# Value products of single units flushed one at a time, and indexer scores rectified in place in PSUM

## The chip, the cores and the metric

The kernel runs on one core of a Trainium2 chip. The metric is the device time of one execution, in microseconds. The time of before is the median of three runs; the profile is of a separate execution. Engines are named as in the profile: PE (TensorE) with its weight loads PEld, DVE (VectorE), ACT (ScalarE), POOL (GpSimd) and SP, which issues transfers.

## What is computed

One layer of a decoder trunk on x of 512 tokens by 1024 channels, in float32. One input projection feeds three causal token mixers. The parts that matter here, cut from the reference:

```python
u = einsum('bsd,de->bse', x, w_in) + b_in          # all projections
# B) sparse attention: an indexer picks 128 keys per query
rel   = relu(einsum('bthd,bsd->bths', iqb, ik))    # 8 index heads of 32
score = einsum('bths,bth->bts', rel, iwb)          # weighted sum over heads
_, idx = top_k(where(causal, score, NEG), topk)
o_b = softmax(q k[idx] / 8) v[idx]                 # 8 heads of 64, one key head
# C) compressed-block, selected-block and window branches, gated and summed
o_c = gb[..., 0:1] * o_cmp + gb[..., 1:2] * o_s + gb[..., 2:3] * o_w
# merge, output projection, LayerNorm
m = g[:, :, 0] * (y_a @ w_pa) + g[:, :, 1] * (y_b @ w_pb) + g[:, :, 2] * (y_c @ w_pc)
out = layernorm(ALPHA * x + m @ w_o)
```

A) is a pooling mixer with windows of 2 to 16. With 512 tokens the selected-block branch takes all blocks, so only the indexer's top-k changes which keys are attended.

## The kernel before

Every f32 product is made of three products of a high and a low part (`mm3`, L67 to L70; groups `d`, `pp` and `wo` in the profile). A projection of 128 channels (`dense`) has 8 steps of three matmuls of 128x512. Weights come through `load_w`: a DMA into a staging tile, a copy of the high part on ACT (L93), a subtraction for the low part (L95), on POOL while the attention runs.

PE's instructions stand in the order in which the program issues them (`manual_schedule` for PE). The instructions of the other engines and of the DMA queues are placed by the compiler's own schedule. The program writes PE's order by weaving two things: the attention, and a stream `F` of projections, compressions and merges, of which `F.step(n)` issues the next n steps as filler.

**The indexer.** `index_scores(j)` (L285 to L301) makes the scores of query block j = 1, 2, 3: for each of 8 heads a matmul into a PSUM tile `is` of the pool `pq` (4 buffers of one bank), a rectification on ACT into an SBUF tile `rel` (L292, from the tag `b` with 6 buffers), and a multiply-add on DVE into the sums `acc` (L294 for the first head, L296 for the others). Two filler steps stand after each head. Beside it run the compressions of keys and values (`compress_in`, `bk`, `bkl`; `compress_mid`, `cpk`) and the scale of the values (`vscales`). The top-k on the sums is 16 rounds of `MAX8` and `MATCH_REPLACE8` on DVE for each block (L305, L306), spread over the attention that follows.

**The attention.** Work is cut into units. A "c" unit (group g, query block j, branch br) is a selected-block or window attention; the two branches of one (g, j) add into the same accumulator. A "b" unit (g, j) is the sparse attention of four heads, with an accumulator of its own. There are 16 "c" units, then 8 "b" units in the order b00, b01, b02, b03, b10 to b13 (g, then j). A unit consists of one or two sub-units. `front` (L422) makes the scores `qk` (L442), softmax and the probabilities `p` (L461, L463), and a transposing DMA on SP into `pt` (L470; tag `pt`, 2 buffers). `back` (L472) makes the value products on PE (L480): for each of j + 1 blocks of keys three times two matmuls in f16. `finish` (L533) is one DVE instruction that reads the accumulator and writes `yc` or `yb`.

The two accumulators that take turns (`psum_acc`) are halves of one tile, `ACC`, of 2 KB per partition:

```python
ACC = pv.tile([128, 2, 2, 128], F32, name="acc2")
```

Units whose `front` is issued wait in the list `backs` with the count of sub-units at that time. `flush(limit)` (L781) takes two units at a time, when the second one lies at least LAG = 2 sub-units back, issues both units' `back` and `finish`, then filler steps. At the end `flush(1000)` takes the rest and puts 12 filler steps before each pair.

Of the kernel before, what the change touches and what calls it, by code (L numbers as in the profile page):

```python
# [7 lines left out]
F32 = mybir.dt.float32  # L8
# [26 lines left out]
def trunk(ctx, tc, a, out, dbg=None):  # L35
# [12 lines left out]
    def big(tag, name, dt=F32, shape=(128, 2, 512)):  # L48
        return bp.tile(list(shape), dt, tag=tag, name=name, bufs=BUFS[tag])
# [4 lines left out]
    def dps(name):  # L54
        return pd.tile([128, 512], F32, tag="pd", name=name)

    def qps(name):
        return pq.tile([128, 512], F32, tag="pq", name=name)
# [42 lines left out]
    ps = qps("idle")  # L101
# [183 lines left out]
    def index_scores(j):  # L285
        n = (j + 1) * 128
        acc = cp.tile([128, n], F32, name=f"acc{j}")
        for h in range(8):
            ps = qps(f"is{j}{h}")[:, :n]
            nc.tensor.matmul(ps, QI[h][:, (j - 1) * 128:j * 128], KI[:, :n], start=True, stop=True)  # L290
            rel = big("b", "rel", F32, (128, 512))[:, :n]
            nc.scalar.activation(rel, ps, AF.Relu)  # L292
            if h == 0:
                nc.vector.tensor_scalar(acc, rel, IW[:, j, 0:1], None, op0=OP.mult)  # L294
            else:
                nc.vector.scalar_tensor_tensor(acc, rel, IW[:, j, h:h + 1], acc, op0=OP.mult, op1=OP.add)  # L296
            yield
        dg = acc[:, j * 128:n]
        nc.vector.tensor_add(dg, dg, cmask[:, 384:512])
        dbg(f"score{j}", acc)  # L300
        negm[j] = acc  # L301
# [231 lines left out]
    def finish(acc, j, Z, y):  # L533
        c = slice(j * 128, j * 128 + 128)
        nc.vector.scalar_tensor_tensor(y[:, :, c], acc, yscale, Z[:, :, c], op0=OP.mult, op1=OP.mult)
# [4 lines left out]
    def psum_acc():  # L540

        turn[0] ^= 1
        return ACC[:, turn[0]]
# [105 lines left out]
    def split_y(br, src):  # L649
        YS[br] = []  # L650
        for g in range(2):
            h, l = big("t", f"yh{br}{g}", F32R), big("t", f"yl{br}{g}", F32R)
            split(h, l, src[g])
            YS[br].append((h, l))
# [77 lines left out]
    for n in (2, 1, 1, 1, 1, 1, 2):  # L732
        for _ in range(n):
            st.step()
        for _ in range(n):
# [11 lines left out]
               [(early_g, 2, d) for d in range(1, 4)] +  # L747
               ["c1", (f_qb, 1, 0), (f_qb, 1, 1), (f_zb, 1, 0), (f_zb, 1, 1)] + [(merge, 2, d) for d in range(KT)])
    ix = Stream([(index_scores, j) for j in (1, 2, 3)])
    while ix.step():  # L750
        F.step(2)
# [4 lines left out]
    def tk(n):  # L756
        tkn[0] += n
        while rounds and tkn[0] >= 1:
            tkn[0] -= 1
            fn, j = rounds.pop(0)  # L760
            fn(j)

    def tk_until(j):
        while (topk_end, j) in rounds:
            fn, i = rounds.pop(0)
            fn(i)
# [10 lines left out]
    backs = []  # L777
    accs, cmps = {}, {}
    nsub = 0

    def flush(limit):  # L781

        while backs and (limit == 1000 or len(backs) > 1 and backs[1][0] <= limit):
            pair, n = backs[:2], 0
            del backs[:2]
            if limit == 1000:
                F.step(12)
            for _, un, (kind, g, j, br) in pair:
                if kind == "c":
                    F.until(("vscales",), ("compress_v",), ("f_zc", g, 0), ("f_zc", g, 1))  # L790
                else:
                    F.until(("f_zb", g, 0), ("f_zb", g, 1))
            for _, un, (kind, g, j, br) in pair:
                for _ in un.back(br == 0):
                    n += 1
                if kind == "b":
                    finish(un.acc, j, zb[g], YB[g])
                elif br == 1:
                    cmps[g, j].back(un.acc)
                    finish(un.acc, j, zc[g], YC[g])  # L800
                    if j == 0:
                        flags.add(f"c{g}")
                        if g == 1:
                            split_y(2, YC)
            F.step(0.3 * n)

    for w in work:
        kind, g, j, br = w
        if kind == "c":
            if br == 0:  # L810
                accs[w[:3]] = psum_acc()
            F.until(("compress_k",), *([("f_kk", g)] if g else []), *([("f_qc", g, e) for e in range(2)] if g else []))
            if j == 3 and br == 0:
                YC.append(big("t", f"yc{g}"))
            gv = GS[:, j, :].rearrange("p (h b) -> p h b", b=3)
            if br == 0:
                cmps[g, j] = Compressed(g)
            un = Unit(f"c{g}{j}{br}", accs[w[:3]], j, qc[g], kk[g][br], cmask[:, (3 - j) * 128:],
                      1 + 2 * br + g, gv[:, 4 * g:4 * g + 4, 1 + br], None if br else cmps[g, j])
        else:  # L820
            F.until(("f_qb", g, 0), ("f_qb", g, 1))
            if j == 0:
                YB.append(big("t", f"yb{g}"))
            if j:
                tk_until(j)
            un = Unit(f"b{g}{j}", psum_acc(), j, qb[g], KB[0], cmask[:, 384:] if j == 0 else negm[j],
                      0, None)
        for u in range(un.nsub):
            for _ in un.front(u):
                F.step(3.25)  # L830
            with tc.issue_after(un.last.ins):
                tk(1.7)
            nsub += 1
            F.step(2)
            flush(nsub - LAG)
        backs.append((nsub, un, w))
    flush(1000)
    F.rest()
    POOL[0] = False
# [60 lines left out]
    for t in range(NT):  # L900
        last = t == NT - 1
        for c0, c1 in ((512, 768), (768, 1024)) if last else ((512, 1024),):
            ps = dps("wo")
# [14 lines left out]
        if not last:  # L918
            c = cs.pop()
# [82 lines left out]
```

## Time and profile before

| | |
|---|---|
| median of 3 runs | 537.79 us (534.98 to 538.72) |
| the profiled execution | 536.65 us |
| its span, first to last instruction | 534.9 us |
| PE busy | 510.4 us |
| DVE / ACT / POOL busy | 380.2 / 278.4 / 218.5 us |
| mean granted TensorE clock | 0.982 of 2.4 GHz |

Busy time of PE counts modelled ends of pipelined matmuls; the start times of successive matmuls are the better measure inside a stretch. Idle time of an engine is put down to the instruction that released it.

### The profile page before, as it was taken

The page shows a single profiled execution, that of the slowest core. Times are in us where ns is not written, and L with a number is a line of the kernel's source. Part 1 is how long each engine was busy: PE and PEld are TensorE (multiplying, and loading weights), DVE is VectorE, ACT ScalarE, POOL GpSimd, SP SyncE. Part 2 cuts the span into 40 slices and gives each one's busy share as a digit, 9 for nine tenths or more (in the row PEclk, how much of TensorE's full clock was granted, in tenths as well). Part 3 has the DMA queues.
Part 4 walks back from the last instruction along what each step waited for, and adds up shares of the span by engine and source line. Part 5 has one row for each costly group of instructions (what it writes and reads, how often), then busy time and mean ns, then how long its engine had stood idle before and what let it go on. Part 6 is the DMA issues. An engine that isn't in the chain of part 4 may idle for free. (4 is left out here: it accounts for less than half of the span.)

```text
span 534.9 us, 7764 instructions
## 1 busy us (share of the span) xinstructions
PE 510.4 (95%) x2718; PEld 423.7 (79%) x2718; DVE 380.2 (71%) x928; ACT 278.4 (52%) x561; POOL 218.5 (41%) x190
## 2 busy tenths in 40 slices
PE   8999999999999998999998995999899999999993
PEld 5899878888888886788887884887787888887883
DVE  5774798898769898997898879565653345554276
ACT  6783465667655666565546564575553245342000
POOL 0425433436553756153534534227651212116043
PEclk9999989999999999999999998899999999999997
DMA  8622331363854434364545636256444435463012
GB/s 286 256 79 80 112 126 60 87 148 86 183 139 123 119 85 117 63 181 124 140 121 104 132 110 145 49 138 138 119 119 134 141 137 187 148 205 110 1 69 89
DMA packets 82135, 66.72 MB, mean 125 GB/s; under 512 B 67184, under 2 KB 68656, under 8 KB 82096
## 3 DMA queue, kind: packets, MB, share of 16 engines
q1 hardware_dynamic: 74912, 40.54, 28.5%
q0 software_dynamic: 7184, 25.69, 16.1%
q8 instruction: 21, 0.34, 0.3%
q14 instruction: 18, 0.15, 0.1%
HBM read 47.87 MB, written 2.10 MB: 93 GB/s over the span
## 5 line engine op out<-in xcount | busy, mean ns | idle before, releaser
L68 PE MATMUL d<-xh,w_h 128*128 128x512 f32 (+1 forms) x424 | 167.5, 395 | 2.6 <-ACT z L153 2.2
L69 PE MATMUL d<-xl,w_h 128*128 128x512 f32 (+1 forms) x424 | 165.8, 391 | 0.0
L70 PE MATMUL d<-xh,w_l 128*128 128x512 f32 (+1 forms) x424 | 165.5, 390 | 0.0
L95 POOL TENSOR_TENSOR w_l<-w_st,w_h 128x1024 fp32r<-128x1024 f32 x41 | 99.5, 2428 | 127.1 <-ACT w_h L93 120.4
L68 PEld LDWEIGHTS d<-xh,w_h 128*128 128x128 f32 x424 | 80.5, 190 | 18.3 <-ACT z L153 2.6
L70 PEld LDWEIGHTS d<-xh,w_l 128*128 128x128 f32 x424 | 80.3, 189 | 16.9
L69 PEld LDWEIGHTS d<-xl,w_h 128*128 128x128 f32 x424 | 80.4, 190 | 14.1
L93 ACT ACTIVATE w_h<-w_st 128x1024 fp32r<-128x1024 f32 x53 | 56.2, 1060 | 36.9 <-DMA w_st<-in_wt_dram 20.5
L449 ACT ACTIVATE qkc<-qkc,nb 128x512 f32<-128x512 f32 (+3 forms) x64 | 32.0, 501 | 49.8 <-DVE nb L444 32.0
L95 POOL TENSOR_TENSOR wp_l<-wp_st,wp_h 128x512 fp32r<-128x512 f32 x16 | 20.8, 1297 | 48.3 <-ACT wp_h L93 48.3
L641 POOL TENSOR_TENSOR m<-m,tg 128x512 f32<-128x512 f32 x12 | 17.5, 1457 | 54.2 <-DVE tg L615 54.0
L463 DVE SCALAR_TENSOR_TENSOR pc<-qkc,r,pc 128x512 f16<-128x512 f32 (+3 forms) x64 | 32.4, 544 | 8.2 <-ACT pc L461 7.9
L461 ACT ACTIVATE pc<-qkc,r 128x512 f16<-128x512 f32 (+3 forms) x64 | 29.5, 525 | 15.1 <-DVE r L457 7.2
L444 DVE CUSTOM_DVE_ANT_0 qkc<-qkc,cmask 128x512 f32<-128x512 f32 (+3 forms) x64 | 31.2, 493 | 2.9 <-PE qkc L442 2.5
L449 ACT ACTIVATE qkb<-qkb,nb 128x128 f32<-128x128 f32 (+3 forms) x32 | 16.0, 499 | 23.1 <-DVE nb L444 22.8
L92 POOL DMA_DIRECT2D w_st<-in_wt_dram x41 | 23.3, 569 | 9.9 <-POOL w_l L95 5.9
L70 PE MATMUL wo<-woh,ml 128*128 128x512 f32 (+1 forms) x72 | 26.4, 367 | 0.6 <-DVE ml L65 0.6
L69 PE MATMUL wo<-wol,mh 128*128 128x512 f32 (+1 forms) x72 | 26.3, 366 | 0.0
L68 PE MATMUL wo<-woh,mh 128*128 128x512 f32 (+1 forms) x72 | 26.3, 365 | 0.0
L306 DVE MATCH_REPLACE8 acc<-m,acc 128x256 f32<-128x256 f32 (+2 forms) x48 | 25.9, 541 | 0.0
L305 DVE MAX8 m<-acc 128x8 f32<-128x256 f32 (+2 forms) x48 | 25.2, 548 | 0.1
L68 PE MATMUL pp<-yh,wp_h 128*128 128x512 f32 x64 | 25.1, 392 | 0.0
(249 smaller groups left out, 1015.3 us busy)
## 6 DMA issues: line engine op xcount, KB each, us to landing
w_st<-in_wt_dram POOLq DMA_DIRECT2D x41, 512.0 KB, 3.7
w_st<-in_wt_dram SPq DMA_DIRECT2D x12, 512.0 KB, 4.4
wp_st<-in_wp_dram POOLq DMA_DIRECT2D x16, 256.0 KB, 3.0
wo_st<-in_wo_dram SPq DMA_DIRECT2D x8, 512.0 KB, 3.5
xst<-in_xT_dram SPq DMA_DIRECT2D x8, 256.0 KB, 4.8
wp_st<-in_wp_dram SPq DMA_DIRECT2D x8, 256.0 KB, 2.6
z<-in_x_dram SPq DMA_DIRECT2D x4, 512.0 KB, 5.1
wvst<-in_wve_dram SPq DMA_DIRECT2D x4, 320.0 KB, 7.1
```

The lines of the kernel that those rows point to most:

```text
L68: nc.tensor.matmul(ps, wh, rh, start=start, stop=False)
L69: nc.tensor.matmul(ps, wh, rl, start=False, stop=False)
L70: nc.tensor.matmul(ps, wl, rh, start=False, stop=stop)
L92: (nc.gpsimd if POOL[0] else nc.sync).dma_start(st, src)
L93: nc.scalar.activation(h[:, :n], st, AF.Copy)
L95: eng.tensor_sub(l[:, :n], st, f(h[:, :n]))
L305: nc.vector.max(m8, negm[j])
L306: nc.vector.match_replace(negm[j], m8, negm[j], MARK)
L444: nc.vector.tensor_tensor_reduce(sc[i], sc[i], self.mask, -0.125, 3e38, OP.add, OP.min, nb[:, i:i + 1])
L449: nc.scalar.activation(sc[i], sc[i], AF.Exp, scale=-1.0, bias=nb[:, i:i + 1], accum_out=den[:, i:i + 1])
L461: nc.scalar.activation(p[:, 0, i], sc[i], AF.Copy, scale=r[:, i:i + 1])
L463: self.last = nc.vector.scalar_tensor_tensor(p[:, 1, i], sc[i], r[:, i:i + 1], p[:, 0, i], op0=OP.mult, op1=OP.subtract)
```

## The change

`flush` takes two units only where the kind is "c", whose two units share an accumulator; a "b" unit is flushed alone, as soon as it lies two sub-units back. The filler steps ahead of a group in the last flush are 8 in place of 12. In `index_scores` the rectified score is written over the score in its PSUM tile instead of into `rel` in SBUF.

```diff
@@ index_scores
             nc.tensor.matmul(ps, QI[h][:, (j - 1) * 128:j * 128], KI[:, :n], start=True, stop=True)
-            rel = big("b", "rel", F32, (128, 512))[:, :n]
+            rel = ps
             nc.scalar.activation(rel, ps, AF.Relu)
@@ flush
-        while backs and (limit == 1000 or len(backs) > 1 and backs[1][0] <= limit):
-            pair, n = backs[:2], 0
-            del backs[:2]
+        while backs and (limit == 1000 or len(backs) >= backs[0][3] and backs[backs[0][3] - 1][0] <= limit):
+            pair, n = backs[:backs[0][3]], 0
+            del backs[:len(pair)]
             if limit == 1000:
-                F.step(12)
-            for _, un, (kind, g, j, br) in pair:
+                F.step(8)
+            for _, un, (kind, g, j, br), _ in pair:
...
-            for _, un, (kind, g, j, br) in pair:
+            for _, un, (kind, g, j, br), _ in pair:
@@ the loop over the units
-        backs.append((nsub, un, w))
+        backs.append((nsub, un, w, 2 if kind == "c" else 1))
```

## Rows read from the trace of the kernel before

**Rows 1.** The page, busy time of each engine and its share of the span.

```profile
PE 510.4 (95%) x2718; PEld 423.7 (79%) x2718; DVE 380.2 (71%) x928; ACT 278.4 (52%) x561; POOL 218.5 (41%) x190
```

**Rows 2.** PE's waits: us in total, times, longest us.

```profile
PE acc L480 <- DVE yb L535: 8.0, 4, 5.5
PE d L68 <- ACT z L153: 2.2, 1, 2.2
...
PE cpk L69 <- DVE bkl L65: 1.2, 1, 1.2
...
PE wo L70 <- DVE ml L65: 0.6, 1, 0.6
```

**Rows 3.** Windows of 20 us: PE, PEld, DVE, ACT, POOL busy, granted clock, DMA.

```profile
60.00:80.00 20.00, 18.84 (x114) 15.96 (x113) 19.23 (x28) 11.97 (x20) 8.22 (x6) 0.91 0.40 132
...
320.00:340.00 20.00, 14.55 (x71) 11.55 (x70) 15.25 (x34) 8.65 (x19) 5.86 (x4) 0.83 0.56 126
```

**Rows 4.** PE's timeline, first pair of "b" units: start, length, line, operands.

```profile
328.22 0.28 PE L480 MATMUL acc<-ptb,vh 128*64 128x256 f16 x2
333.95 0.42 PE L480 MATMUL acc<-ptb,vh 128*64 128x256 f16 x2 [5.45 <-DVE yb L535]
...
337.64 0.39 PE L68 MATMUL d<-xh,w_h 128*128 128x512 f32 x1
```

**Rows 5.** PE's timeline, third pair of "b" units.

```profile
382.21 0.28 PE L480 MATMUL acc<-ptb,vh 128*64 128x256 f16 x2
383.91 0.30 PE L480 MATMUL acc<-ptb,vh 128*64 128x256 f16 x2 [1.42 <-DVE yb L535]
...
385.95 0.39 PE L68 MATMUL d<-xh,w_h 128*128 128x512 f32 x1
```

**Rows 6.** PE's timeline, last pair of "b" units.

```profile
405.44 0.39 PE L70 MATMUL d<-xh,w_l 128*128 128x512 f32 x1
...
406.12 0.39 PE L70 MATMUL d<-xh,w_l 128*128 128x512 f32 x1
406.44 0.30 PE L480 MATMUL acc<-ptb,vh 128*64 128x256 f16 x2
...
408.20 0.30 PE L480 MATMUL acc<-ptb,vh 128*64 128x256 f16 x2 [0.58 <-DVE yb L535]
...
409.39 0.30 PE L480 MATMUL acc<-ptb,vh 128*64 128x256 f16 x2
...
409.96 0.39 PE L69 MATMUL d<-xl,w_h 128*128 128x512 f32 x1
```

**Rows 7.** DVE's timeline, the read of the first "b" unit's sums.

```profile
333.43 0.47 DVE L535 SCALAR_TENSOR_TENSOR yb<-acc,yscale,zb 128x256 f32<-128x256 f32 x1
```

**Rows 8.** PE's second score of b02; the last transpose on SP; its time to landing.

```profile
321.03 0.51 PE L442 MATMUL qkb<-kb,bq 128*128 128x384 f32 x2
...
400.06 1.56 SPq L470 DMA_TRANSPOSE ptb<-pb  x1
...
ptb<-pb SPq DMA_TRANSPOSE x1, 3.6
```

**Rows 9.** DVE's and POOL's timelines in the index stage.

```profile
57.38 0.48 DVE L296 SCALAR_TENSOR_TENSOR acc<-rel,iw,acc 128x256 f32<-128x256 f32 x1 [1.02 <-ACT rel L292]
...
59.54 2.46 DVE L296 SCALAR_TENSOR_TENSOR acc<-rel,iw,acc 128x256 f32<-128x256 f32 x1
...
72.58 2.98 DVE L334 SCALAR_TENSOR_TENSOR bk<-d,bias,small 64x496 f32<-64x496 f32 x4
...
59.33 2.39 POOL L95 TENSOR_TENSOR w_l<-w_st,w_h 128x1024 fp32r<-128x1024 f32 x1 [4.24 <-ACT w_h L93]
...
72.39 2.40 POOL L95 TENSOR_TENSOR w_l<-w_st,w_h 128x1024 fp32r<-128x1024 f32 x1 [3.49 <-ACT w_h L93]
```

**Rows 10.** PE's 12th index score; DVE's step for the 8th.

```profile
68.28 0.34 PE L290 MATMUL is<-ki,qi 128*128 128x384 f32 x1
...
67.97 0.49 DVE L296 SCALAR_TENSOR_TENSOR acc<-rel,iw,acc 128x256 f32<-128x256 f32 x1
```

## The prediction

> **What bounds the kernel now.** I read the page's busy table first: TensorE (PE) is busy for 95% of the span [rows 1], so time can only come out of PE's idle stretches and out of stretches at a low granted clock. PE's program order is fixed by hand, so whatever one of its instructions waits for delays everything behind it. The second view is the list of PE's waits [rows 2]: the largest entry is a value product (`acc`, L480) waiting for a VectorE read of the accumulator (`yb`, L535), 8.0 us in 4 waits, the longest 5.5. The others are single waits of 2.2 and 1.2 us. Third, the windows of 20 us [rows 3]: in 320:340 PE is busy for 14.55 us and its clock averages 0.83; in 60:80 there is a small dip of the same kind (18.84 us, 0.91). Fourth, PE's timeline at the four waits [rows 4 to 6]: each lies between two groups of products of one pair of "b" units. PE issues the first unit's products, then must wait until VectorE (DVE) has read that unit's sums, since the second unit's sums lie in the other half of the same bank-sized tile. All four come before 410 us, and later there is one PE wait of 0.6 us (`wo`, on `ml`) [rows 2], so what is saved should reach the end.
>
> **Edit 1, "b" units flushed singly: what it removes.** Products of one group start 0.054 us apart (24 products from 408.20 to the last pair at 409.39: 1.19/22) [rows 6]. The pair at 328.22 should thus be followed at 328.33, and the next one starts at 333.95: a gap of 5.62, 0.17 more than the 5.45 that the row gives as idle [rows 4]. The pair at 382.21 gives 1.59 against 1.42, again 0.17 [rows 5]. Four gaps are therefore 8.0 + 4 x 0.17 = 8.7 us. The long one also costs clock: after it, PE's 12 products, 2 scores and 3 projection matmuls take from 333.95 to 337.64, 3.69 us [rows 4], while the same seventeen after the short gap take from 383.91 to 385.95, 2.04 us [rows 5]. That is 1.65 us at the lower of the two clock levels. Removed in all: 8.7 + 1.65 = 10.35 us.
>
> **What it adds.** Four pairs become eight stretches, so four more changes between f32 projections and f16 products. Three projection matmuls take 0.68 us (405.44 to 406.12), 0.227 each. Entering a stretch costs 406.44 - 406.12 - 0.227 = 0.09; leaving it, from the last pair at 409.39 to the second f32 matmul at 409.96, costs 0.57 - 0.11 - 0.227 = 0.23 [rows 6]. That is 0.32 each and 1.3 us for four. Bounds: zero, if these pauses exist inside the old gaps too, and twice 0.32 each. I take 1.3.
>
> **What it moves.** The first unit's products of each pair go one sub-unit forward. Unit b00 now has them just before the score matmul of 321.03 [rows 8], and b01 keeps about its old place at 328. So some 7 us of projections lie between them. What decides is when DVE reads b00's sums. In the old order that read ran at 333.43, 5.1 us after the products ended at 328.33, because DVE was behind with top-k and softmax work [rows 4, 7]. With the same lag the read would begin at 321.4 + 5.1 = 326.5 and end before 328: no wait left, with 1 us to spare. The remaining pairs had gaps of 1.59 and 0.75, so DVE was hardly behind there, and their new distance is again a sub-unit of about 6 us. If a read is late, all of PE's stream queues behind that product. The early products issue no transfer, but they free the buffer for the next unit's transposed probabilities sooner; the transposing DMAs on SP can only move forward. Their own inputs are in place: the last unit's transpose is issued at 400.06 and takes 3.6 us, so it lands at 403.7, 2.7 us ahead of its group's start at 406.44 [rows 6, 8]. There the new order has b12's 18 products and 0.9 step in between but 8 steps in place of 12. That is 3.1 steps of 0.68 less and 1.3 us more (18 x 0.054 + 0.32), 0.8 us less cover out of 2.7: still enough. If that cover failed, the price would be the shortfall alone. The number of steps before the end of the filler stream is the same in sum, only spread differently: nothing.
>
> **Edit 2, the rectified scores stay in PSUM.** Nothing is removed from PE. ScalarE writes, and DVE reads, a PSUM tile instead of an SBUF one, 24 times, and each of the four PSUM buffers is held until DVE is done instead of until ScalarE is done. No row shows this very form, so I bound it. DVE's step on 256 columns takes 0.48 us from SBUF [rows 9]. A step with its input in PSUM ran at 2.98/4 = 0.75 us for 496 columns, which is the same rate with a fixed part. So the duration stays. One of the 24, at 59.54, took 2.46 us: it began 0.2 us after a GpSimd subtraction of 2.39 us (59.33 to 61.72) and ended 0.3 after it. Yet the four steps with PSUM input at 72.58 lay beside just such a subtraction (72.39 to 74.79) and were not held up [rows 9].
>
> The Trainium skill, "SBUF — State Buffer", section "Who interferes with whom", says that a VectorE instruction with two SBUF inputs shares a read port with GpSimd while one with a single SBUF input does not; both rows agree. By this rule the held-up step would fall from 2.46 to 0.48 us; without it edit 2 would give nothing.
>
> What hangs on that step is the scale of the values, then the weights of the compression, and then PE's 1.2 us wait for `bkl` [rows 2]. Gain at most: that wait and the clock beside it, 1.2 + 0.09 x 20 = 3.0 us [rows 2, 3]. Against it stands the held buffer: score n+4 must wait for DVE's step n. The closest place in the old trace: the 12th score starts at 68.28, and the 8th score's step begins at 67.97 and lasts 0.49, so it would free the buffer at 68.46, 0.2 us too late [rows 10]. Loss with DVE's order unchanged: 0.2 us, which the wait for `bkl` then absorbs. Since DVE is the late engine there, PE can't run far ahead even if that wait goes. I take a gain of 1.0, nearer to the middle of (-3.0, +0.2) than to its best end.
>
> The Trainium skill's "PSUM — Partial Sum Buffer", summary for kernel authors, advises to evacuate promptly, which speaks against this edit; the trace of before, where the buffers go free earlier, shows no PE wait for one, and by the rows above the price would be 0.2 us.
>
> **Sum.** The profiled execution took 536.65 us (span 534.9 and 1.75 around it). 536.65 - 8.7 - 1.65 + 1.3 - 1.0 = 526.6. The median of the runs, 537.79, lies 1.14 above the profiled one, so the forecast for the median is 527.7 us.
>
> **Rivals.** (a) *The reads stay late.* The compiler places DVE's instructions by its own schedule. If b00's read stays where it is, behind the probabilities of b02, PE waits at b01 as now and only the 3.1 us of the three short gaps go, less 1.3: with edit 2 some 535. For it: the read stood 5.1 us behind its products. Against it: a read that is ready 7 us sooner has an earlier place in any order by readiness. It decides once the read starts more than 6.6 us after its products.
> (b) *The gain is given back elsewhere.* Every queue but PE's is laid out anew, and the c stage has waits of 2.2 us and less [rows 2] that can grow as well as vanish; two such waits with their clock (2.2 + 1.65 each) give back 7.7 us, 535.4, with a spread from 530 to 538. For it: DVE is busy for 19.23 of 20 us in 60:80 [rows 3], and a small delay shows. Against: a new wait is as likely to replace an old one as to come on top.
> (c) *Slower: the score buffers.* If DVE's new order puts two of its four-step groups (2.98 us each) before a score's step, PE stops for some 6 us behind the held buffer, and the clock falls for another 1.65. Twice (keys and values) that is 15.3 us, less 9.1: 544. It decides from about 3 us of stop at both places. For it: the buffer is already 0.2 us late at one place [rows 10]. Against: elsewhere in that stage PE keeps its distance.
>
> **How the numbers follow.** Forecast 0.70, (a) 0.11, (b) 0.12, (c) 0.07. One per cent is 5.4 us, about what a measurement can tell from no change; the forecast is faster by more, and so is a part of (b) (0.04), the rest of (b) and (a) lie within 1%, (c) is slower. So faster 0.74, same 0.19, slower 0.07. The range: downward, edit 2's full 3.0 in place of 1.0 and the c stage's 2.2 us wait with its clock gone as well (3.9) give 521.8, rounded to 522. Upward, the doubled price of the stretches gives 529, and the near part of (b) is taken in up to 534.
>
> **What would show it.** Right: no PE wait on `yb` above 0.5 us, PE at full clock in 320:340, eight separate groups of `ptb` products, the step of 2.46 us gone. Wrong: a wait for `yb` or for a DVE score step at the head of PE's list, or PE idle after 410.

## The result and the profile after

The changed kernel takes 529.92 us (median of 4 runs, 529.0 to 530.22) against 537.38 for the kernel before (median of 4): ratio 0.9861, 95% interval 0.9824 to 0.9898. It is faster by over 1% here; measured again (e8_after_again below) the ratio is 0.9892 (0.9867 to 0.9917). The forecast was 527.7, in a range of 522 to 534. The profiled execution took 529.68 us, 7.0 less than that of before; the forecast's sum for it was 526.6, so 3.1 us of the expected gain did not come. Where they went is the question of the experiments.

First the lines that answer to rows of before. PE's busy time has hardly moved, but its share of the shorter span is 97% [rows 1]:

```profile
PE 509.5 (97%) x2718; PEld 421.0 (80%) x2718; DVE 380.4 (72%) x928; ACT 278.6 (53%) x561; POOL 214.7 (41%) x190
```

PE's waits after the change (us in total, times, longest):

```profile
PE d L68 <- ACT z L153: 3.5, 1, 3.5
...
PE wo L70 <- DVE ml L65: 0.6, 1, 0.6
PE qkc L442 <- DVE pc L463: 0.5, 1, 0.5
PE cpk L69 <- DVE bkl L65: 0.4, 1, 0.4
```

The entry of 8.0 us for `yb` [rows 2] is gone altogether, `bkl` fell from 1.2 to 0.4. But `z` rose from 2.2 to 3.5, and a wait of 0.5 on `pc` is new. The windows (PE, PEld, DVE, ACT, POOL busy, granted clock, DMA):

```profile
60.00:80.00 20.00, 19.51 (x122) 16.12 (x121) 18.70 (x32) 13.97 (x25) 8.88 (x6) 1.00 0.39 132
...
320.00:340.00 20.00, 20.00 (x102) 15.91 (x101) 18.57 (x48) 13.56 (x26) 9.43 (x7) 1.00 0.61 133
```

Both windows of rows 3 now show the clock at its upper level throughout (0.91 and 0.83 before). The timeline of PE at the first two "b" units and DVE's read of the first:

```profile
323.13 0.30 PE L480 MATMUL acc<-ptb,vh 128*64 128x256 f16 x2
...
323.38 0.28 PE L480 MATMUL acc<-ptb,vh 128*64 128x256 f16 x2
323.58 0.62 PE L442 MATMUL qkb<-kb,bq 128*128 128x384 f32 x2
...
330.65 0.30 PE L480 MATMUL acc<-ptb,vh 128*64 128x256 f16 x2
...
325.95 0.47 DVE L535 SCALAR_TENSOR_TENSOR yb<-acc,yscale,zb 128x256 f32<-128x256 f32 x1
```

Unit b00's products end near 323.5, DVE reads its sums at 325.95 to 326.42, and b01's products come at 330.65: 4.2 us of room where PE had waited 5.45 us [rows 4].

To see where the rest went, the span is cut at four places of PE's order: the first index score (`is`), the first score of a "c" unit (a compressed-block score, `sc`), the first of a "b" unit (`qkb`), and the last output product (`wo`). Each column is the time from one cut to the next, the last one the place of the last `wo`. In us, from the profiled executions:

| kernel | start | index | c | b and tail | last `wo` at |
|---|---|---|---|---|---|
| before | 52.15 | 39.94 | 207.03 | 226.63 | 525.75 |
| after | 53.10 | 38.45 | 209.58 | 217.57 | 518.70 |
| difference | +0.95 | -1.49 | +2.55 | -9.06 | -7.05 |

The b stage gave back what was forecast. The c stage, which neither edit touches by name, became 2.55 us longer. Its trace shows one DVE step that grew, the second half of a SiLU (`silu2`, L408). Before, it ended just ahead of a GpSimd subtraction:

```profile
130.22 0.69 DVE L408 SCALAR_TENSOR_TENSOR zc<-zc,z 128x512 f32<-128x512 f32 x1
130.82 0.08 DVE L306 MATCH_VALUE_LOAD acc<-m,acc 128x8 f32 x1
130.89 0.41 DVE L306 MATCH_REPLACE8 acc<-m,acc 128x256 f32<-128x256 f32 x1
...
130.88 2.40 POOL L95 TENSOR_TENSOR w_l<-w_st,w_h 128x1024 fp32r<-128x1024 f32 x1 [4.17 <-ACT w_h L93]
```

In the changed kernel the compiler's order has the two top-k instructions in front of it. They cost it 0.4 us; its old place also lies 0.5 us later against the subtraction (130.87 against 131.06, before 130.22 against 130.88). So it begins 0.2 us after the subtraction's start, and ends 0.55 us after the subtraction's end:

```profile
130.87 0.09 DVE L306 MATCH_VALUE_LOAD acc<-m,acc 128x8 f32 x1
130.94 0.41 DVE L306 MATCH_REPLACE8 acc<-m,acc 128x256 f32<-128x256 f32 x1
131.27 2.73 DVE L408 SCALAR_TENSOR_TENSOR zc<-zc,z 128x512 f32<-128x512 f32 x1
...
131.06 2.39 POOL L95 TENSOR_TENSOR w_l<-w_st,w_h 128x1024 fp32r<-128x1024 f32 x1 [4.16 <-ACT w_h L93]
```

It has two SBUF inputs, `zc` and `z`, like the step of 2.46 us in rows 9. PE pays for it only later. Its instructions in this stage are the same in both kernels, and up to 191 us they keep the same distance from the stage's start within 0.1 us. DVE meanwhile stays 2.1 us late, as its read for the third "c" accumulator shows (before, then after):

```profile
195.94 0.48 DVE L535 SCALAR_TENSOR_TENSOR yc<-acc,yscale,zc 128x256 f32<-128x256 f32 x1
...
198.05 0.48 DVE L535 SCALAR_TENSOR_TENSOR yc<-acc,yscale,zc 128x256 f32<-128x256 f32 x1
```

From 199 us on PE meets that lateness: first at the new wait on `pc`, then at the longer wait for `z`, after which it runs longer at the lower clock. PE's timeline, and the window around it (before, then after):

```profile
210.94 0.51 PE L68 MATMUL d<-xh,w_h 128*128 128x512 f32 x1 [2.21 <-ACT z L153]
...
218.59 0.62 PE L442 MATMUL qkc<-kw,cq 128*128 128x512 f32 x2
...
210.00:220.00 10.00, 8.84 (x31) 6.84 (x32) 9.57 (x24) 5.88 (x13) 3.47 (x5) 0.83 0.45 106
```

```profile
213.04 0.79 PE L68 MATMUL d<-xh,w_h 128*128 128x512 f32 x1 [3.55 <-ACT z L153]
...
221.96 0.62 PE L442 MATMUL qkc<-kw,cq 128*128 128x512 f32 x2
...
210.00:220.00 10.00, 6.96 (x18) 5.47 (x19) 8.81 (x21) 5.14 (x11) 5.56 (x9) 0.66 0.53 124
```

The wait is 1.34 us longer, and the same instructions behind it take 8.92 us instead of 7.65, at a mean granted clock of 0.66 against 0.83 in the window. With 1.2 us around the wait on `pc`, PE is 3.9 us late at 222, counted from the stage's start; some 1.4 us come back by the stage's end, in part because a wait of 0.4 us on `tg` at 282 is gone. The theory for the experiments: edit 1 is worth its 9 us in the b stage; edit 2 saves about 1 us in the index stage and, by reordering DVE's queue, runs this step into the subtraction, which costs 2.5 us in the c stage. The rivals: the new order of the products costs the c stage something; or the stage lengths vary by chance.

### The profile page after: what moved, and what is told of

The parts are those of the page before. It is cut to its first block, busy times and chain, and to the rows that moved or that the text cites. A ratio compares the mean times of both kernels' runs of the same rounds, so it can differ in the third digit from the quotient of the medians.

```text
span 527.9 us, 7758 instructions
## 1 busy us (share of the span) xinstructions
PE 509.5 (97%) x2718; PEld 421.0 (80%) x2718; DVE 380.4 (72%) x928; ACT 278.6 (53%) x561; POOL 214.7 (41%) x190
## 4 chain that ended last, share of the span: by engine, by line
PE 53%; DVE 3%; DMA 2%; ACT 1%; issue 0%; DVEq 0%; ACTq 0%
PE d L68 9%; PE d L69 9%; PE d L70 9%; PE pp L68 4%; PE pp L69 4%; PE pp L70 4%; PE acc L480 3%; PE wo L70 3%; PE wo L69 2%; PE wo L68 2%; PE qkb L442 2%; DMA wo_st<-in_wo_dram 2%; PE qkc L442 1%; PE acc L530 1%; DVE wol L65 0%
## 5 line engine op out<-in xcount | busy, mean ns | idle before, releaser
L95 POOL TENSOR_TENSOR w_l<-w_st,w_h 128x1024 fp32r<-128x1024 f32 x41 | 98.1, 2393 | 119.9 <-ACT w_h L93 119.3
L95 DVE TENSOR_TENSOR w_l<-w_st,w_h 128x1024 fp32r<-128x1024 f32 x12 | 16.1, 1347 | 12.8 <-ACT w_h L93 12.8
```

Source lines behind the costliest of these rows:

```text
L95: eng.tensor_sub(l[:, :n], st, f(h[:, :n]))
```

## The experiments

All of the kernels compute the whole result. The ledger of all profiled executions, beside each kernel's median and its ratio to the kernel before (95% interval):

| kernel | start | index | c | b and tail | median us | ratio |
|---|---|---|---|---|---|---|
| e1_single | 52.51 | 38.64 | 207.01 | 217.25 | 527.06 | 0.9825 (0.9788 to 0.9862) |
| e2_psum | 52.15 | 38.37 | 209.54 | 227.54 | 538.24 | 1.0024 (1.0005 to 1.0044) |
| e3_pair_reads | 50.98 | 38.62 | 209.53 | 217.46 | 528.55 | 0.9848 (0.9816 to 0.988) |
| e4_gate_psum | 52.24 | 38.62 | 207.08 | 220.75 | 528.61 | 0.9839 (0.9802 to 0.9876) |
| e5_split_more | 50.77 | 38.60 | 209.65 | 222.11 | 532.88 | 0.9933 (0.9909 to 0.9958) |
| e6_pair_sbuf | 51.76 | 39.97 | 206.95 | 218.33 | 529.62 | 0.9851 (0.9815 to 0.9888) |
| e7_gate_sbuf | 53.57 | 39.47 | 206.79 | 217.79 | 528.43 | 0.9846 (0.9822 to 0.9871) |
| e8_after_again | 53.01 | 38.24 | 209.61 | 219.66 | 531.53 | 0.9892 (0.9867 to 0.9917) |
| e9_single_again | 51.58 | 41.31 | 206.86 | 218.29 | 528.95 | 0.9844 (0.9815 to 0.9872) |
| e10_gate_psum_again | 52.23 | 38.28 | 206.96 | 218.31 | 526.66 | 0.9806 (0.9779 to 0.9833) |

The start varies from 50.77 to 53.57 us over these and does not sort by edit; its +0.95 in the comparison above is not put down to the change.

**Each edit alone.** e1_single takes the changed kernel and puts the rectified scores back into SBUF; e2_psum does the opposite, the kernel before with edit 2 only.

```diff
e1_single, against after
-            rel = ps
+            rel = big("b", "rel", F32, (128, 512))[:, :n]
e2_psum, against before
-            rel = big("b", "rel", F32, (128, 512))[:, :n]
+            rel = ps
```

> Edit 1 alone: 'b' units flushed singly, the rectified scores in SBUF as before. Theory: the change's time is a ledger of four stretches that add up. Up to the b stage every queue has the order of before, so the index stage and the c stage are as before (the gate step at 131 us not held up, the wait on z 2.2 us), and the b stage gives 9.1 us: 9.1 less than before, some 528.3, which is less than with both edits. Rival: the 2.5 us that the c stage lost with both edits are chance or belong to edit 1; then this runs at 530 or above, with the longer wait on z.

> Edit 2 alone: scores rectified in PSUM, 'b' units flushed in pairs as before. Theory: index stage 1.5 us shorter, then VectorE's new order puts the gate step (zc, line 408) next to a GpSimd subtraction, it takes 2.7 us instead of 0.7, and the wait on z grows: in sum 0 to 1.5 us slower than before, 537 to 539, with the four waits on yb (8 us) still there. Rival: edit 2 is a gain by itself and the c stage's loss is chance: 535 to 536.

PE's waits in e1_single, and the SiLU step on DVE's timeline:

```profile
PE d L68 <- ACT z L153: 2.2, 1, 2.2
...
PE cpk L69 <- DVE bkl L65: 1.0, 1, 1.0
```

```profile
129.30 0.69 DVE L408 SCALAR_TENSOR_TENSOR zc<-zc,z 128x512 f32<-128x512 f32 x1
```

The same two views of e2_psum:

```profile
PE acc L480 <- DVE yb L535: 8.1, 4, 5.5
PE d L68 <- ACT z L153: 3.6, 1, 3.6
```

```profile
130.23 2.72 DVE L408 SCALAR_TENSOR_TENSOR zc<-zc,z 128x512 f32<-128x512 f32 x1
```

The four waits on `yb` go with edit 1 and only with it; its b stage is 217.25 against 226.63, -9.38. The held SiLU step and the longer wait for `z` come with edit 2 and only with it. Edit 2 alone makes the kernel slower, by 0.24% or 1.3 us by the ratio (0.3 to 2.4 by its interval; the two medians, 538.24 and 537.45, stand 0.8 apart): index 38.37 against 39.94, c 209.54 against 207.03.

**Is it the split, or the read between the two groups?** e3_pair_reads keeps edit 2 and the pairs with their 12 steps, and issues the products of both "b" units before the read of either.

```diff
e3_pair_reads, against before, beside edit 2
-                    finish(un.acc, j, zb[g], YB[g])
+                    reads.append((un.acc, j, zb[g], YB[g]))
...
+            for r in reads:
+                finish(*r)
```

> Edit 2 kept; 'b' units flushed in pairs as before, but both units' products are issued before either read of the sums. Theory: the wait was for the read that stood between the two groups, nothing else; with the read moved behind both, no wait on yb is left and only four stretches instead of eight are paid: 1.3 us less than the changed kernel, some 528.6. Rival: splitting is what helps (the second unit's inputs or its bank are late however the reads stand): waits of several us at the second groups remain, 533 to 538.

No wait on `yb` is left here either, and the b stage takes 217.46, as in the changed kernel (217.57). So what PE waited for was the read that the program had put between the two units' products; one flush per unit is one way to move it, and this is another. Why the second unit's products, which write the other half of the tile, wait for that read at all is not shown: no kernel here gave the halves tiles of their own. The first pair on PE's timeline (before, then e3_pair_reads), and DVE's two reads behind it:

```profile
327.97 0.30 PE L480 MATMUL acc<-ptb,vh 128*64 128x256 f16 x2
...
337.64 0.39 PE L68 MATMUL d<-xh,w_h 128*128 128x512 f32 x1
```

```profile
327.99 0.30 PE L480 MATMUL acc<-ptb,vh 128*64 128x256 f16 x2
...
330.35 0.39 PE L68 MATMUL d<-xh,w_h 128*128 128x512 f32 x1
...
333.52 0.86 DVE L535 SCALAR_TENSOR_TENSOR yb<-acc,yscale,zb 128x256 f32<-128x256 f32 x2
```

The same instructions take 2.36 us instead of 9.67, though DVE reads the first sums as late as before (333.52 against 333.43). That is 7.31 us less, where the prediction had 5.62 of gap and 1.65 of clock, 7.27. The other three pairs, timed from their first product to the first instruction after their last, give 0.78, 1.62 and 0.78: 10.5 us in all. The b stage gained only 9.17: the four stretches that the pairs save, worth 1.3 us by the prediction, don't show, because a new wait of that size stands in PE's list (the median, 528.55, met the forecast of 528.6, but by a shorter start):

```profile
PE qkb L442 <- DVE pb L463: 1.2, 1, 1.2
```

**The held step given one SBUF input.** In e4_gate_psum, the changed kernel, this one gate's tanh stays in PSUM, so that the SiLU step reads `d` from PSUM and only `z` from SBUF. The copy of `z`, which also reads the PSUM tile, is issued ahead of it.

```diff
e4_gate_psum, against after (silu2)
+        th = ps if i == I_CZ + 2 else dst
...
-            nc.scalar.activation(dst, ps, AF.Tanh, scale=0.5, bias=bhalf[:, i:i + 1])
-            hi(z, ps, b)
-        nc.vector.scalar_tensor_tensor(dst, dst, 1.0, z, op0=OP.add, op1=OP.mult)
+            if th is ps:
+                hi(z, ps, b)
+            nc.scalar.activation(th, ps, AF.Tanh, scale=0.5, bias=bhalf[:, i:i + 1])
+            if th is dst:
+                hi(z, ps, b)
+        nc.vector.scalar_tensor_tensor(dst, th, 1.0, z, op0=OP.add, op1=OP.mult)
```

> The changed kernel with one edit: the gate step that was held up at 131 us takes its tanh from PSUM instead of SBUF, so it has one SBUF input. Theory: it takes 0.7 us again instead of 2.7, VectorE is 2 us less late through the c stage, the wait on z falls from 3.5 to some 2 us or less and its clock loss with it: 2 to 3 us less than the changed kernel, 527 to 528. Rival: VectorE's lateness comes from elsewhere or is made again by the next held-up step: no difference, 529 to 531.

DVE's and POOL's timelines of e4_gate_psum:

```profile
130.25 0.41 DVE L306 MATCH_REPLACE8 acc<-m,acc 128x256 f32<-128x256 f32 x1
130.57 0.68 DVE L412 SCALAR_TENSOR_TENSOR zc<-d,z 128x512 f32<-128x512 f32 x1
...
130.37 2.40 POOL L95 TENSOR_TENSOR w_l<-w_st,w_h 128x1024 fp32r<-128x1024 f32 x1 [4.17 <-ACT w_h L93]
```

The step stands at the same place, again 0.2 us behind the start of the subtraction, and now takes 0.68 us in place of 2.73. The c stage is back at 207.08, the wait for `z` at 2.3, and the wait on `pc` is gone. That settles the cause of the c stage's loss. The Trainium skill, "SBUF — State Buffer", section "Who interferes with whom", gives the rule behind it: a VectorE instruction with two SBUF inputs contends with a GpSimd instruction that reads SBUF, one with a single SBUF input does not. The pair 2.73 and 0.68 agrees. In this profile the b stage took 220.75, with waits of 0.8 for `mh` and 1.1 for `ml` at the output products, so the total did not show the gain; e10 below is the same kernel again.

**The price of a stretch.** e5_split_more issues one filler step between every two blocks of a "b" unit's products in the changed kernel: 12 more stretches, the same instructions.

```diff
e5_split_more, against after
-                for _ in un.back(br == 0):
+                for k, _ in enumerate(un.back(br == 0)):
...
+                    if kind == "b" and k < j:
+                        F.step(1)
```

> The changed kernel, with one more filler step issued between every two key blocks of a b unit's products, so that each block's f16 products stand in a stretch of their own between f32 ones: 12 more stretches, the same instructions otherwise. Theory (a change of type between f32 and f16 matmuls costs the 0.32 us of the prediction, and TensorE is the bound there): the b stage to the last output product grows by 12 x 0.32 = 3.8 us, from 217.6 to about 221.4, and the time goes from 529.9 to about 533.7, ratio to before 0.993. Rival (the cost of a stretch lies in its neighbours and more stretches cost nothing): 217.6 as in the changed kernel, time 529.9, ratio 0.986.

The b stage grew from 217.57 to 222.11, 4.54 us or 0.38 per stretch. Over all seven profiles with this b stage (217.25 to 220.75, 218.52 in the mean) the growth is 3.6 us or 0.30; by the ratios to the kernel before (0.9933 against 0.9861, and 0.9892 for the changed kernel run again) the cost is 2.2 to 3.9 us. PE's timeline shows one of the new stretches by itself:

```profile
328.54 0.30 PE L480 MATMUL acc<-ptb,vh 128*64 128x256 f16 x2
...
328.99 0.50 PE L68 MATMUL d<-xh,w_h 128*128 128x512 f32 x1
...
329.88 0.30 PE L480 MATMUL acc<-ptb,vh 128*64 128x256 f16 x2
```

From one f16 group to the next are 1.34 us; six products at 0.054 and three f32 matmuls at 0.227 make 1.00 of them, so one way out and back in costs 0.34. The price is near the 0.32 taken; the rival, no cost, falls.

**The scores, apart from the grouping.** e6_pair_sbuf is e3_pair_reads with the scores in SBUF, e7_gate_sbuf is e4_gate_psum with the scores in SBUF; the one line changed in each is that of e1_single.

> The kernel before with one line moved: the b units stay in pairs, but both units' products are issued before either unit's read; the rectified scores stay in SBUF. Theory (the lost time was the read between the two units' products, and what the edit on the scores costs in the c stage has nothing to do with how the b units are grouped): no wait for yb on TensorE, c stage 207.0 us and not 209.5, b stage 217.5, time as e1_single, 527 (526 to 528), ratio 0.982. Rival (the c stage's 2.5 us come with the new b order or by chance): c stage 209.5, time 529.5, ratio 0.985.

> The products split as in the changed kernel, the rectified scores in SBUF, and the one gate whose tanh is kept in PSUM as in e4_gate_psum. Theory (the gate's edit only guards a step that here does not stand beside a GpSimd subtraction; the 3.2 us that e4_gate_psum lost late in the b stage were late loads of that one execution): c stage 207.0, b stage 217.4, time as e1_single, 527 (526 to 528), ratio 0.982. Rival (the gate's edit itself costs the waits for mh and ml late in the b stage): b stage 220.7, time 530, ratio 0.986.

Both have the c stage of the kernel before (206.95 and 206.79), so the loss there belongs to edit 2, however the "b" units are grouped, and the gate's edit adds nothing of its own (b stage 217.79). Nor is the step's place a matter of chance: in all five profiles with the scores in SBUF it begins 0.7 us ahead of the subtraction, and in all seven with the scores in PSUM 0.2 us behind its start. The medians, 529.62 and 528.43, lie above what was expected. e6's six runs spread from 524.91 to 531.19, and its index stage was 39.97 with the clock at 0.91 in 60:80, so its median alone would not have told the theories apart; the stages do.

**Three kernels side by side on one chip.**

> The changed kernel itself once more, to stand beside the next two on one chip. Theory (edit 2 costs the c stage 2.5 us and saves the index stage about 1, whatever the chip): c stage 209.5, 529.5 (528.5 to 530.5). Rival (what divides the kernels is chance of the run, not the edit): c stage anywhere between 207 and 209.5, and medians of all three within 0.5 us.

> The edit of the products alone, scores in SBUF, as e1_single. Theory: c stage 207.0, index stage 38.6 to 40.0, time 1.5 us below e8_after_again, 528 (527 to 529). Rival: within 0.5 us of e8_after_again.

> As e4_gate_psum: both edits, and the one gate step kept off the shared port. Theory: c stage 207.1 and index stage 38.5, so 2.5 us below e8_after_again and 1 us below e9_single_again, 527 (526 to 528); the two late waits for mh and ml of that earlier profile gone. Rival (the gate's edit costs something late in the b stage): the waits for mh and ml are there again, and the time is that of e8_after_again.

The medians are 531.53 (530.24 to 532.43), 528.95 (526.1 to 530.63) and 526.66 (525.26 to 528.45), in the expected order with steps of 2.6 and 2.3 us; the first was expected 1 us lower, and the index stage of the second, 41.31, lies above its expected 38.6 to 40.0. The c stage is 209.61 in the first and 206.86 and 206.96 in the others. The wait for `mh` of e4's profile is gone in e10 and the one for `ml` is not (1.4 us; it is 0.3 to 1.4 over all these profiles). So both edits with the one gate step kept out of the way beat the changed kernel, by 4.9 us here. Of these the c stage gives 2.65; the rest stands in the start and the b stage, which vary between runs of one kernel, and in the first measurements the ratios (0.9839 for e4 against 0.9861) don't part the two. Against e1_single it is not settled: 528.61 and 526.66 against 527.06 and 528.95 in the two comparisons.

## Why the prediction was right, and where not

**What bounds the kernel** stood. The four waits and the clock behind them were what the b stage could give back, and what was saved there reached the end.

**Edit 1** was right in its size: 8.7 of gaps and 1.65 of clock less 1.3 for stretches is 9.05 us; the b stage gave 9.06, and with edit 1 alone 9.38. That agreement is closer than the measure: run again, the same two kernels gave 6.97 and 8.34. Over the seven profiles with single flushes and no other change in the b stage it takes 217.25 to 220.75, 218.52 in the mean, against 226.63 and 227.54 in the two with the old order, so the gain is 8.6 us by the means. What varies lies late, in short waits before and at the output products. What was to be seen was seen: no wait on `yb`, eight separate groups, full clock in 320:340. The price of a stretch is 0.34 by the row rather than 0.32, which is 0.1 us in the sum of four. What the four waits cost, gaps and clock together, is 10.5 us by e3's rows, where 10.35 was taken.

**What edit 1 moves**: the read was expected at 5.1 us behind its products and ready in time with about 1 us to spare. It came some 2.5 us behind them, with 4.2 to spare. Rival (a), the late reads, fell.

**Edit 2** is the step that failed: "I take a gain of 1.0", from bounds of -3.0 to +0.2. The index stage was understood. The step of 2.46 us became one of 0.48 beside a running subtraction:

```profile
60.50 0.48 DVE L296 SCALAR_TENSOR_TENSOR acc<-is,iw,acc 128x256 f32<-128x256 f32 x1
...
61.94 2.22 DVE L247 SCALAR_TENSOR_TENSOR vl<-v,vscale,vh 128x640 f16<-128x640 f32 x2 [0.37 <-ACT vh L246]
...
60.28 2.40 POOL L95 TENSOR_TENSOR w_l<-w_st,w_h 128x1024 fp32r<-128x1024 f32 x1 [4.19 <-ACT w_h L93]
```

Part of the gain passed on at once: the next step with two SBUF inputs, `vl`, now began before the subtraction's end and took 2.22 where it had taken 1.69. The wait for `bkl` is 0.2 to 0.6 us in the seven profiles with edit 2 and 0.9 to 1.5 in the five without it. The index stage is 38.2 to 38.6 us in the seven, with the clock at 1.00 in 60:80, and 38.6 to 41.3 in the five, where that clock was 0.84 or 0.91 in three and 1.00 in two. The mean gain is 1.4 us (39.87 less 38.45). Against the two at full clock the gain is 0.2 and 1.0, so a part of the 1.4 is clock, and the runs don't show how much of that the edit brings about. A second SiLU step, at 85.56 before, is free of a subtraction too in the seven (0.67 to 0.68 us against 1.82 to 2.00 in the five); what it is worth to PE isn't shown. But the bounds held only that stage. The edit moved two instructions on DVE in the c stage, a step ran into a subtraction, and 2.55 us were lost. The rows showed the risk: a step with two SBUF inputs that begins just behind a subtraction is held until it ends, and rows 9 had one such step. I applied the rule to the step that the edit freed and not to the other steps that a new order could bring in. In sum edit 2 costs 1.3 us by e2's ratio, against the gain of 1.0.

**Rivals.** (b), the gain given back in the c stage, was right in kind: the wait that grew is the 2.2 us for `z` that it named, and clock went with it, 1.27 us behind the wait where 1.65 had been added. The second place was the smaller one, 1.2 us around `pc`, and 1.4 came back: 2.55 of the 7.7 us. (c), stops behind the held score buffers, fell: no profile with edit 2 has PE waiting for a score's step, and the index stage became shorter.

**The sum.** 526.6 expected and 529.68 measured in the profile: +2.55 in the c stage, +0.95 in the start, -0.49 for an index gain of 1.49 where 1.0 was taken, and under 0.1 in the rest. The range held because its upper end had been drawn for rival (b).

## What to carry to other kernels

Where two halves of an accumulator take turns, issue the read of the first only after the products of the second, or put other work between them: the read in the middle is a wait in the tensor engine's fixed order. An edit to one engine's operands can reorder a queue that a compiler lays out, far from the edit; list beforehand which VectorE steps with two SBUF inputs stand within a fraction of a microsecond of a long GpSimd instruction, since such a step lost 2.0 of the instruction's 2.4 us here. And look far behind the place: what VectorE lost at 131 us, PE paid from 199 us on. When a change of several parts falls short of its sum, cut the span at a few fixed instructions and compare stage by stage; times of one kernel that spread over up to 6.3 us could not have told these parts apart.

## What the runs showed of the hardware that was not expected

A shift of 0.9 us against GpSimd, 0.4 of it the two top-k instructions put in front, cost 2.04 us on one step (2.73 against 0.69) and 2.55 us in PE's c stage: the step that starts 0.2 us behind the subtraction waits until it ends, and the one that ended as it started lost nothing. And in e5_split_more a short stretch of f16 products among f32 ones costs PE 0.34 us on its own timeline, at a granted clock of 1.00 in 320:340.
